# Expert sums in ordered groups, W1's first half in 1 MB loads, and gates behind the one-hot, in a two-block fp32 forward pass

## Chip, cores and metric

The kernel runs on one core of one Trainium2 chip. The metric is the device time of one execution in microseconds.

## What is computed

Two transformer blocks on 512 tokens of width 1024, all in fp32. Only a part of the first block and its hand-over to the second matter here: the hierarchical mixture of experts.

```python
def hier_moe(x, w_group, b_group, w_expert, b_expert, w1, w3, w2):
    ...
    g_logits = (xf @ w_group + b_group).astype(jnp.float32)
    g_sel = jnp.argmax(g_logits, axis=-1)
    ...
    e_top, e_loc = lax.top_k(e_logits, TOP_K_INNER)
    gate = (g_w * jax.nn.softmax(e_top, axis=-1)).reshape(-1)
    ...
        hid = jax.nn.silu(xb @ w1[e]) * (xb @ w3[e])
        return hid @ w2[e]
    ...
    out = jax.ops.segment_sum(ys * row_gate[:, None], row_tok, num_segments=T)
```

There are 4 groups of 8 experts; each token takes 2 experts of one group. An expert has w1 and w3 of 1024 x 512 and w2 of 512 x 1024. The block ends in `h + g2 * hier_moe(...)` and a norm by `final_g`; the second block begins with a layer norm (`ln_in_g_2`, `ln_in_b_2`) and a product with `w_in_2`.

## The kernel before

The program is one long stream per engine. A scheduler sets the order of each engine's instructions from the order in the code, from dependences and from priorities; tiles come from pools that are rings by tag (PG 24 buffers of 512 KB over all partitions, RAW 3 of 1 MB, WH and WL 3 each of 512 KB, SG, SA and PT small ones). A load into a ring waits until the ring's oldest buffer has been read. All loads are issued by SyncE (SP), in order; the gathers of token rows by GpSimd (POOL).

**Mix and norm (L1038 to L1063).** `ev_mix` takes each 128x512 result of the mix product, scales it by g1R and adds it to h on VectorE (DVE), takes the norm's sums, and multiplies h by the row scale sc2R on POOL (L1048). `modulated` then finishes u on DVE and `logits` stores it to u_d (L1063).

**Routing (L1068 to L1213).** Maxima over the logits give the one-hot oh of the two experts of each token. A triangular product gives the rank of each token within its expert; `cnt` and `cnti` hold the largest count. Gates come from sigmoids (ge, gate), and are split into a rounded high part gth and a rest gtl. `slots` (L1153 on) compares ranks with iota to get the one-hot R (L1165); R times pay gives the token of each slot (slots, L1169, then sz, ids, tok), and R times payg its gate (slotg, L1181, then sg, gts in L1183 to L1186). `pair_gather` fetches token rows by tok (L1266). Every engine reads cnti into a register (L1420) and passes a branch (L1424) for the case that an expert has over 64 tokens, which falls back to a loop over single experts (`expert_in`, `expert_out`).

**Experts in pairs (L1367 to L1405, main loop at L1449).** 16 pairs of experts; the first takes columns 0 to 63 of PSUM's partitions, the second 64 to 127. `pair_in` multiplies by W1 and then W3, each in four steps q of two k-slices; the raws of a step are 512 KB per expert, in tags PG, PG, WH, WL. `both` issues the two half-height matmuls (L1371, tile e). After each step it takes one piece of the `beside` stream, the sums of the pair before: `combine` in `outputs` multiplies the yl and yh of that pair by the placing one-hot (L1301, L1302, tile cmb) and adds to h (L1303). `pair_tokens` transposes the next pair's rows (xgt, L1364), `pair_loads` issues the eight w2r loads (L1396, tag PG), `pair_out` transposes the hidden rows (hdt, L1404, copied to hp by ScalarE (ACT), L1406), multiplies by w2r (also L1371), and `outputs` scales the result by gate and g2R (y, L1292) and splits it into yh and yl (L139 on ACT, L140 on DVE).

**End of the loop (j = 16).** The loads of fgR, lng and lnb, and `nav_weights(0).prepare()`, which loads the first raws of the second block's product nav and splits them (L139, L140), stand in the code ahead of the loads and matmuls of w2r of pair 15. Then come the last sums, and the norm chain of the second block: h times fgR (L1939), its statistics, h by lng and lnb (L1223, L1225), transposes xt (L1242) and nav's products.

## Time and profile before

| | |
|---|---|
| median of 3 runs | 3155.69 us (3153.24 to 3157.79) |
| the profiled execution | 3154.16 us, its span 3152.4 us |
| TensorE (PE) | 94% busy, granted clock 0.984 |
| DVE, ACT, POOL | 59%, 36%, 9% busy |
| DMA | 534.17 MB, 527.46 of it on the queue of SP's loads |

The span is cut by the trace into engines' busy times. PE is nearly always busy, but a busy PE isn't one at its peak rate; the loop over the experts runs from about 660 to 1205 us. The table of the profile that shows the span in 40 slices has the transfers at 353 to 377 GB/s in just this stretch, and at 60 to 290 GB/s elsewhere. Times in the rows are in us, unless they are called ns; L is a line of the kernel; `SPq` and `DVEq` are the engines' instruction queues.

### The profile page before, as it was taken

The numbers are of one execution on the slowest core, as the hardware profiler recorded it, in microseconds if no ns is written. First come the engines' busy times: TensorE is split into PE (matmuls) and PEld (weight loads), VectorE is DVE, ScalarE is ACT, GpSimd is POOL, SyncE is SP. The second block draws the span as 40 slices with busy tenths as digits, with TensorE's granted clock in tenths as the row PEclk, the third lists the DMA queues.
The fourth block names the chain that finished last, engine by engine and source line by source line (L and its number), as shares of the span: only waits on it lengthen the run. The fifth ranks groups of instructions, "written<-read, shape, count | busy, mean of one in ns | idle before, by whom it ended". The sixth has DMA issues, their size and how long they took to land.

```text
span 3152.4 us, 36476 instructions
## 1 busy us (share of the span) xinstructions
PE 2970.1 (94%) x13749; PEld 2204.3 (70%) x13749; DVE 1848.6 (59%) x3521; ACT 1131.5 (36%) x1986; POOL 279.6 (9%) x263
## 2 busy tenths in 40 slices
PE   6988999979999998999999999999999999999998
PEld 5766777733333335878867788888888876788887
DVE  6899888633223227555589754434545588764434
ACT  4555244210000003444567332222444576432221
POOL 2133000300000000221000200000221000200000
PEclk9989999989999999999999999999999999999999
DMA  6222756679999995432233623243433234632341
GB/s 222 92 90 65 233 185 195 208 289 353 362 372 377 358 376 193 137 114 94 76 112 111 231 100 107 92 142 100 147 117 101 79 99 116 225 107 93 107 139 62
DMA packets 296257, 534.17 MB, mean 169 GB/s; under 512 B 30279, under 2 KB 172789, under 8 KB 296071
## 3 DMA queue, kind: packets, MB, share of 16 engines
q1 hardware_dynamic: 293480, 527.46, 48.5%
q0 software_dynamic: 2304, 4.20, 0.5%
q8 instruction: 110, 1.80, 0.2%
q14 instruction: 77, 0.62, 0.1%
q10 hardware_dynamic: 286, 0.09, 0.0%
HBM read 486.50 MB, written 44.38 MB: 168 GB/s over the span
## 4 chain that ended last, share of the span: by engine, by line
PE 64%; DVE 7%; issue 3%; DMA 2%; ACT 2%; POOL 1%; SPq 0%; DVEq 0%; POOLq 0%; ACTq 0%
PE e L1371 12%; PE fm L292 9%; PE fm L295 9%; PE fm L293 9%; PE ffo L295 2%; PE ffo L293 2%; PE ffo L292 2%; PE cmb L1301 1%; PE cmb L1302 1%; POOL tl L1634 1%; DVE xT L140 1%; DMA w2r<-in_moe_w_dram 1%; PE mix L292 1%; PE mix L295 1%; PE mix L293 1%
## 5 line engine op out<-in xcount | busy, mean ns | idle before, releaser
L140 DVE TENSOR_TENSOR wl<-raw,wh 128x1024 fp32r<-128x1024 f32 (+3 forms) x403 | 462.3, 1149 | 313.8 <-ACT wh L139 312.2
L139 ACT CAST wh<-raw 128x1024 fp32r<-128x1024 f32 (+3 forms) x403 | 388.6, 966 | 543.0 <-PE fm L295 224.2
L292 PE MATMUL fm<-xT,wh 128*128 128x512 f32 (+1 forms) x1264 | 481.9, 384 | 0.0
L293 PE MATMUL fm<-xT,wl 128*128 128x512 f32 (+1 forms) x1264 | 479.9, 382 | 1.3 <-DVE wl L140 1.3
L295 PE MATMUL fm<-xT,wh 128*128 128x512 f32 (+1 forms) x1264 | 301.9, 381 | 0.0
L1371 PE MATMUL e<-w,xx 128*64 128x512 f32 x1024 | 293.8, 605 | 0.0
L293 PEld LDWEIGHTS fm<-xT,wl 128*128 128x128 f32 x1264 | 238.2, 188 | 46.7 <-DVE wl L140 1.7
L292 PEld LDWEIGHTS fm<-xT,wh 128*128 128x128 f32 x1264 | 238.2, 189 | 45.1
L295 PEld LDWEIGHTS fm<-xT,wh 128*128 128x128 f32 x1264 | 231.6, 188 | 45.5
L1371 PEld LDWEIGHTS e<-w,xx 128*64 128x64 f32 x1024 | 79.2, 137 | 138.6 <-issue 130.0
L293 PE MATMUL fm<-uT,wl 128*128 128x512 f32 (+1 forms) x360 | 145.3, 403 | 3.8 <-DVE wl L140 3.8
L1303 DVE TENSOR_TENSOR h<-h,cmb 128x512 f32<-128x512 f32 x128 | 84.6, 686 | 109.2 <-PE cmb L1302 108.5
L1371 PE MATMUL e<-w2r,hp 128*64 128x512 f32 x512 | 141.9, 607 | 3.6 <-DMA w2r<-in_moe_w_dram 2.1
L292 PE MATMUL fm<-uT,wh 128*128 128x512 f32 (+1 forms) x360 | 145.0, 404 | 0.0
L292 PE MATMUL ffo<-wl,hid 128*128 128x512 f32 x352 | 137.1, 390 | 0.0
L293 PE MATMUL ffo<-wh,hid 128*128 128x512 f32 x352 | 136.9, 389 | 0.0
L1371 PEld LDWEIGHTS e<-w2r,hp 128*64 128x64 f32 x512 | 52.8, 137 | 87.9 <-issue 64.5
L1921 DVE SCALAR_TENSOR_TENSOR ffs<-ffs,fm 128x512 f32<-128x512 f32 x44 | 30.3, 688 | 137.7 <-ACT ffs L1920 137.7
L295 PE MATMUL ffo<-wh,hid 128*128 128x512 f32 x352 | 108.4, 389 | 0.0
L139 ACT CAST yh<-y 128x512 fp32r<-128x512 f32 x32 | 19.8, 618 | 224.2 <-DVE y L1292 224.2
L1923 DVE SCALAR_TENSOR_TENSOR ffs<-ffs,fm 128x512 f32<-128x512 f32 x44 | 30.3, 688 | 114.4 <-PE fm L295 114.4
L1634 POOL TENSOR_TENSOR tl<-ml,tl 128x512 f32<-128x512 f32 x32 | 47.7, 1497 | 554.3 <-DVE tl L1630 540.6
(603 smaller groups left out, 5955.6 us busy)
## 6 DMA issues: line engine op xcount, KB each, us to landing
w<-in_moe_w_dram SPq DMA_DIRECT2D x256, 512.0 KB
raw<-in_w_in_dram SPq DMA_DIRECT2D x71, 1024.0 KB
w2r<-in_moe_w_dram SPq DMA_DIRECT2D x128, 512.0 KB
raw<-in_w_ffn_in_dram SPq DMA_DIRECT2D x44, 1024.0 KB
raw<-in_w_mod_dram SPq DMA_DIRECT2D x42, 512.0 KB
raw<-in_w_ffn_out_dram SPq DMA_DIRECT2D x20, 1024.0 KB
raw<-in_w_out_dram SPq DMA_DIRECT2D x12, 1024.0 KB
t_d<-bg SPq DMA_DIRECT2D x48, 256.0 KB
```

The costliest lines, as they stand in the source:

```text
L139: S.copy(hi, src)
L140: (eng or V).tensor_tensor(lo, src, f(hi), OP.subtract)
L292: PE.matmul(ps, l[0], r[1], start=start and n == 0, stop=False)
L293: PE.matmul(ps, l[1], r[0], start=False, stop=False)
L295: PE.matmul(ps, l[0], r[0], start=False, stop=stop and n == len(pairs) - 1)
L1301: PE.matmul(ps, pl, yl[:, cs], start=True, stop=False)
L1302: PE.matmul(ps, pl, yh[:, cs], start=False, stop=True)
L1303: V.tensor_tensor(h1[i][m], h1[i][m], ps, OP.add)
L1371: PE.matmul(ps[hs], lhs[:, hs], rhs[h], start=start, stop=stop)
L1634: G.tensor_tensor(th, m, th, OP.add)
L1921: V.scalar_tensor_tensor(s, s, 1.0, pgt, OP.add, OP.mult)
L1923: V.scalar_tensor_tensor(s, s, 0.5, pup, OP.mult, OP.mult)
```

## The change

1. In `ev_mix` the row scale by sc2R moves from POOL to DVE.
2. In the routing, `behind(ins, first)` adds an ordering without a wait between two instructions of one engine. With it pay stands behind the one-hot's sum ob, and cnt, ge (and with it the gates) and ex stand behind R. So cnti, the gates and payg come behind R in DVE's order.
3. `combine` becomes a generator that can be sent a matmul behind which its next sum has to stand. `pair_in` asks for 3, 0 | 3, 0, 2, 0 banks of sums after the steps (a bank is two cmb matmuls) in place of one after each step.
4. `pair_in` loads W1 as one 1 MB raw per expert (tag RAW, four k-slices) and two of 512 KB (PG), and W3 as PG, PG, WH, WL. Ahead of the routing's branch SP's order has now 3 loads of 1 MB and 20 of 512 KB for the pairs, before 20 of 512 KB. `expert_in` and `expert_out` in the branch give up RAW for SG and SA buffers.
5. At j = 16 the w2r loads of pair 15 come first; then, pinned in the code's order, fgR, lng, lnb and nav's raws; `prepare` stands behind `pair_out`.

```diff
+    def behind(ins, first):
+
+        tc.add_manual_dep(ins.ins, first.ins.name, mybir.DependencyInfo(mybir.DependencyClass.NoSync, mybir.DependencyReason.DATA),
+                          reason="order")
+        return ins
...
             if hf == 0:
                 hss[i] = pt_("u2", F32, (128, 1024))
-            G.tensor_tensor(hss[i][:, cs], h1[i][hf], sc2R[:, cs], OP.mult)
+            V.tensor_tensor(hss[i][:, cs], h1[i][hf], sc2R[:, cs], OP.mult)
...
-    V.tensor_tensor(ob, oh[:, :, 0], oh[:, :, 1], OP.add)
+    obi = V.tensor_tensor(ob, oh[:, :, 0], oh[:, :, 1], OP.add)
...
-    cnt = const("cnt", [128, 1])
-    V.tensor_reduce(cnt, ps[:, 128:160], AX, OP.max)
-    cnti = const("cnti", [128, 1], I32)
-    V.tensor_copy(cnti, cnt)
+    cntp = ps[:, 128:160]
...
-        V.tensor_tensor(pay[:, :, j], oh[:, :, j], bc(aid[:, :, j], 32), OP.mult)
+        behind(V.tensor_tensor(pay[:, :, j], oh[:, :, j], bc(aid[:, :, j], 32), OP.mult), obi)
...
-            V.tensor_tensor(R[:, :, o:o + n], iota[:, 0:n].unsqueeze(1).to_broadcast([128, 8, n]),
+            Ri = V.tensor_tensor(R[:, :, o:o + n], iota[:, 0:n].unsqueeze(1).to_broadcast([128, 8, n]),
...
-    tok0, ids0, gt0, gates0 = slots(slot_tiles[0], 0, True)
+        return tok, ids, gt, gates, Ri
+
+    tok0, ids0, gt0, gates0, R0i = slots(slot_tiles[0], 0, True)
+    cnt = const("cnt", [128, 1])
+    behind(V.tensor_reduce(cnt, cntp, AX, OP.max), R0i)
+    cnti = const("cnti", [128, 1], I32)
+    V.tensor_copy(cnti, cnt)
     ge = carve("ge", [128, 4, 4])
-    V.tensor_tensor(ge, gl, bc(gm, 4), OP.subtract)
+    behind(V.tensor_tensor(ge, gl, bc(gm, 4), OP.subtract), R0i)
...
-    V.tensor_tensor(ex, m1, m2, OP.subtract)
+    behind(V.tensor_tensor(ex, m1, m2, OP.subtract), R0i)
...
+            after = yield
             for i in range(4):
                 for m in range(2):
                     cs = slice(m * 512, m * 512 + 512)
                     ps = trp("cmb")
                     pl = place[:, i * 128:(i + 1) * 128]
-                    PE.matmul(ps, pl, yl[:, cs], start=True, stop=False)
+                    mm = PE.matmul(ps, pl, yl[:, cs], start=True, stop=False)
+                    if after is not None:
+                        behind(mm, after)
                     PE.matmul(ps, pl, yh[:, cs], start=False, stop=True)
                     V.tensor_tensor(h1[i][m], h1[i][m], ps, OP.add)
-                    yield
-        return combine()
+                    after = yield
+        sums = combine()
+        next(sums)
+        return sums
...
-            PE.matmul(ps[hs], lhs[:, hs], rhs[h], start=start, stop=stop)
+            mm = PE.matmul(ps[hs], lhs[:, hs], rhs[h], start=start, stop=stop)
+        return mm
 
     def pair_in(j, xT, beside):
+
         pss = []
-        for nm in ("moe_w1", "moe_w3"):
+        for n, nm in enumerate(("moe_w1", "moe_w3")):
             W = [I[nm][0, 2 * j + h].rearrange("(p a) n -> p a n", a=8) for h in range(2)]
             ps = mmp("e1")
-            for q in range(4):
+            k = 0
+            for tag, w, banks in ((("RAW", 4, 0), ("PG", 2, 3), ("PG", 2, 0)), (("PG", 2, 3), ("PG", 2, 0), ("WH", 2, 2), ("WL", 2, 0)))[n]:
                 ws = []
                 for h in range(2):
-                    raw = t_([128, 2, 512], F32, ("PG", "PG", "WH", "WL")[q], "w13")
-                    load(raw, W[h][:, 2 * q:2 * q + 2])
+                    raw = t_([128, w, 512], F32, tag, "w13")
+                    load(raw, W[h][:, k:k + w])
                     ws.append(raw)
-                for k in range(2):
-                    both(ps, xT[:, 2 * q + k], [w[:, k] for w in ws], q + k == 0, q + k == 4)
-                next(beside, None)
+                for m in range(w):
+                    mm = both(ps, xT[:, k + m], [r[:, m] for r in ws], k + m == 0, k + m == 7)
+                k += w
+                if beside:
+                    for b in range(banks):
+                        try:
+                            beside.send(None if b else mm)
+                        except StopIteration:
+                            pass
...
-        if j == 16:
-            fgR = row("fgR", I["final_g"])
-            norm, xT = normalizer(I["ln_in_g_2"], I["ln_in_b_2"], rows_of(xres[0]))
-            nav_tm = nav_weights(0).prepare()
         if prev is not None:
-            for _ in beside:
+            for _ in beside or ():
                 pass
-            beside = pair_out(j - 1, prev, pair_loads(j - 1))
+            ws = pair_loads(j - 1)
+            if j == 16:
+                fgR = row("fgR", I["final_g"], True)
+                norm, xT = normalizer(I["ln_in_g_2"], I["ln_in_b_2"], rows_of(xres[0]))
+                nav_tm = nav_weights(0, True)
+            beside = pair_out(j - 1, prev, ws)
+            if j == 16:
+                nav_tm.prepare()
```

How the order moves, first on PE, in one of the first pairs of the loop (w are raws of its W1, e its product, cmb the sums of the pair before). Before, from the pair's first matmul:

```order
L1371 MATMUL e_1441_7154<-w_1442_7155,xx_7086 64x512
L1301 MATMUL cmb_7163<-yl_7147,place_7143 128x512
L1302 MATMUL cmb_7163<-yh_7146,place_7143 128x512
L1301 MATMUL cmb_7175<-yl_7147,place_7143 128x512
L1371 MATMUL e_1441_7154<-w_1443_7157,xx_7086 64x512
L1371 MATMUL e_1441_7154<-w_1442_7155,xx_7086 64x512
L1371 MATMUL e_1441_7154<-w_1443_7157,xx_7086 64x512
L1302 MATMUL cmb_7175<-yh_7146,place_7143 128x512
L1301 MATMUL cmb_7187<-yl_7147,place_7143 128x512
L1302 MATMUL cmb_7187<-yh_7146,place_7143 128x512
```

Now, from the last of the twelve e matmuls in a row here:

```order
L1386 MATMUL e_1483_7334<-w_1487_7349,xx_7266 64x512
L1312 MATMUL cmb_7355<-yl_7327,place_7323 128x512
L1315 MATMUL cmb_7355<-yh_7326,place_7323 128x512
L1312 MATMUL cmb_7359<-yl_7327,place_7323 128x512
L1315 MATMUL cmb_7359<-yh_7326,place_7323 128x512
L1312 MATMUL cmb_7363<-yl_7327,place_7323 128x512
L1315 MATMUL cmb_7363<-yh_7326,place_7323 128x512
L1386 MATMUL e_1483_7334<-w_1491_7367,xx_7266 64x512
L1386 MATMUL e_1483_7334<-w_1492_7369,xx_7266 64x512
```

The groups of three cmb with one or three e rows between them have become groups of six.

On DVE, between the rank and the register load of the branch. Before, with the last payload payg ahead of R:

```order
L1130 TENSOR_REDUCE cnt<-rank_5534 128x1
L1135 TENSOR_TENSOR rt_5554<-carve_4962,rank_5534 128x256
L1132 CAST cnti<-cnt 128x1
L1213 TENSOR_TENSOR payg<-carve_4962,gtl 128x4x32
L1136 TENSOR_REDUCE rank<-rt_5554 128x8
L1165 TENSOR_TENSOR R_5567<-carve_4962,rank 128x8x64 x2
```

Now, with R some twenty rows further up, the part ahead of the register load of cnti:

```order
L150 TENSOR_TENSOR gtl<-carve_4962,gth 128x8
L1223 TENSOR_TENSOR payg<-carve_4962,gth 128x4x32
L1223 TENSOR_TENSOR payg<-carve_4962,gtl 128x4x32
L1223 TENSOR_TENSOR payg<-carve_4962,gth 128x4x32
L1223 TENSOR_TENSOR payg<-carve_4962,gtl 128x4x32
L1189 COPY sg_5614<-slotg_5605 128x64
L1190 TENSOR_TENSOR sg_5614<-sg_5614 128x32
L1192 COPY gts_5559<-sg_5614 64x16 x2
L1444 TENSOR_LOAD cnti
```

The count, the gates (carve is their page), gth, gtl and the four payloads have moved from ahead of R to a place between R and the gate copies gts, ahead of the register load.

On SP, at the loop's end. Before, the last loads of W2 of pair 14 and what follows:

```order
L1396 DMA w2r_9307<-in_moe_w_dram 128x1024
L979 DMA fgR_9345<-in_final_g_dram 128x1024
L979 DMA lng_9347<-in_ln_in_g_dram 128x1024
L979 DMA lnb_9349<-in_ln_in_b_dram 128x1024
L393 DMA raw_9351<-in_w_in_dram 128x4x512
L393 DMA raw_9353<-in_w_in_dram 128x4x512
L1396 DMA w2r_9399<-in_moe_w_dram 128x1024
L1396 DMA w2r_9401<-in_moe_w_dram 128x1024
```

Now, the last loads of W2 of pair 15 and what follows:

```order
L1420 DMA w2r_9519<-in_moe_w_dram 128x1024
L988 DMA fgR_9521<-in_final_g_dram 128x1024
L988 DMA lng_9523<-in_ln_in_g_dram 128x1024
L988 DMA lnb_9525<-in_ln_in_b_dram 128x1024
L400 DMA raw_9527<-in_w_in_dram 128x4x512
L400 DMA raw_9529<-in_w_in_dram 128x4x512
L348 DMA raw_9938<-in_w_in_dram 128x8x256
```

The eight w2r loads of pair 15, which stood behind the rows of the norm and two raws of nav, now stand ahead of them.

## Rows read from the trace of the kernel before

**Rows 1.** DMA view, 900 to 1100 us; the GB/s line has 40 slices of 5 us.

```profile
GB/s 394 419 406 415 342 229 372 407 411 410 410 351 246 387 405 414 408 410 307 262 389 409 415 407 408 308 261 381 397 415 414 409 283 257 387 419 410 410 410 310
DMA packets 20842, 74.53 MB, mean 373 GB/s; under 512 B 2671, under 2 KB 2671, under 8 KB 20833
```

**Rows 2.** Windows of 2 us in one pair: busy us by engine, PEclk, DMA share, GB/s.

```profile
908.00:910.00 2.00, 2.00 (x8) 0.67 (x6) 0.14 (x1) 0.00 (x0) 0.00 (x0) 1.00 1.04 422
...
924.00:926.00 2.00, 2.00 (x8) 0.81 (x6) 0.97 (x2) 0.00 (x0) 0.00 (x0) 1.00 0.71 193
...
928.00:930.00 2.00, 2.00 (x9) 0.77 (x8) 0.27 (x1) 0.90 (x2) 0.34 (x1) 1.00 0.46 84
```

**Rows 3.** Waits of SP's queue, 640 to 1240 us: total us, times, longest.

```profile
SPq L1382 <- PE e L1371: 166.9, 35, 8.7
```

**Rows 4.** The same view, of 922 to 926 and of 926 to 930 us.

```profile
SPq L1382 <- PE e L1371: 7.3, 1, 7.3
...
SPq L1382 <- PE e L1371: 3.6, 1, 3.6
```

**Rows 5.** PE's timeline of one pair: start, us, engine, line, operation, count, [idle before].

```profile
910.12 1.04 PE L1371 MATMUL e<-w,xx 128*64 128x512 f32 x2
912.12 0.50 PE L1301 MATMUL cmb<-yl,place 128*128 128x512 f32 x1 [0.96 <-DVE yl L140]
...
913.33 1.93 PE L1371 MATMUL e<-w,xx 128*64 128x512 f32 x6
915.19 0.50 PE L1302 MATMUL cmb<-yh,place 128*128 128x512 f32 x1
...
916.08 1.07 PE L1371 MATMUL e<-w,xx 128*64 128x512 f32 x2
...
929.55 7.09 PE L1371 MATMUL e<-w,xx 128*64 128x512 f32 x32
936.47 8.57 PE L1371 MATMUL e<-w2r,hp 128*64 128x512 f32 x32
944.47 1.04 PE L1371 MATMUL e<-w,xx 128*64 128x512 f32 x2
```

**Rows 6.** PE's timeline at pair 0's second product.

```profile
698.55 7.09 PE L1371 MATMUL e<-w2r,hp 128*64 128x512 f32 x32 [0.68 <-ACT hp L1406]
```

**Rows 7.** PE's and DVE's timelines at the loop's end; one window of 10 us.

```profile
1194.82 10.86 PE L1371 MATMUL e<-w2r,hp 128*64 128x512 f32 x32 [2.13 <-DMA w2r<-in_moe_w_dram]
...
1194.29 3.50 DVE L140 TENSOR_TENSOR wl<-raw,wh 128x1024 fp32r<-128x1024 f32 x3 [1.21 <-ACT wh L139]
...
1212.94 1.22 DVE L1939 TENSOR_TENSOR h<-h,fgR 128x1024 f32<-128x1024 f32 x1
...
1210.00:1220.00 10.00, 3.24 (x13) 2.13 (x13) 9.54 (x19) 3.28 (x7) 1.41 (x2) 0.84 0.00 2
```

**Rows 8.** DVE's groups of 600 to 660 us: busy us, mean ns, idle before.

```profile
L1213 DVE TENSOR_TENSOR payg<-carve,gth 128x128 fp32r<-128x128 f32 x2 | 0.6, 284 | 0.0
```

**Rows 9.** Timeline of all engines, 651 to 668 us.

```profile
657.50 0.35 DVE L1186 COPY gts<-sg 64x16 f32<-64x16 f32 x2
...
662.65 4.30 DVE L1285 TENSOR_TENSOR place<-carve,rows 128x512 fp32r<-128x512 f32 x7 [4.80 <-DVEq L1424]
662.66 1.94 PE L1364 MATMUL xgt<-ident,xg 128*128 128x128 f32 x8 [5.76 <-DVEq L1424]
662.73 2.85 SPq L1382 DMA_DIRECT2D w<-in_moe_w_dram  x6
```

**Rows 10.** Line L1424, the branch: ns min/median/max, first and last start.

```profile
L1424 PEldq COMPARE_BRANCH  x1: 3352/3352/3352, 654.0 to 654.0; - x1
...
L1424 DVEq COMPARE_BRANCH  x1: 72/72/72, 658.1 to 658.1; - x1
L1424 DVEq EVENT_SEMAPHORE  x1: 21/21/21, 662.5 to 662.5; - x1
```

**Rows 11.** Line L1048; DVE's groups of 600 to 660 us; one window of 10 us.

```profile
L1048 POOL TENSOR_TENSOR u<-h,sc2R x8: 1279/1290/2372, 602.9 to 632.3; 128x512 f32<-128x512 f32 x8
...
L1043 DVE TENSOR_TENSOR mixt<-mix,g1R 128x512 f32<-128x512 f32 x8 | 5.3, 684 | 3.4 <-PE mix L295 3.4
...
620.00:630.00 10.00, 8.08 (x56) 6.25 (x56) 9.56 (x24) 1.37 (x4) 1.82 (x2) 1.00 0.56 179
```

More of the change, by code (lines that the diff above doesn't have):

```diff
@@ L373, in build, with __init__ @@
     class TM:
-        def __init__(self, kt, W, c0, n, name="tm", lead=0, tail=0):
+        def __init__(self, kt, W, c0, n, name="tm", lead=0, tail=0, pinned=False):
+            self.pinned = pinned
             self.kt, self.W, self.c0, self.n, self.name, self.lead, self.tail = kt, W, c0, n, name, lead, tail
@@ L392, in fetch @@
                 self.raw[k0] = t_([128, g, n], F32, "RAW", "raw")
-                load(self.raw[k0], self.W[k0 * 128:(k0 + g) * 128, self.c0:self.c0 + n].rearrange("(k p) n -> p k n", p=128))
+                ins = load(self.raw[k0], self.W[k0 * 128:(k0 + g) * 128, self.c0:self.c0 + n].rearrange("(k p) n -> p k n", p=128))
+                if self.pinned:
+                    tc.keep_in_program_order(ins)
             return self.raw[k0]
@@ L1186, in gates @@
                 V.tensor_copy(d, s)
-        return tok, ids, gt, gates
-    tok0, ids0, gt0, gates0 = slots(slot_tiles[0], 0, True)
+        return tok, ids, gt, gates, Ri
[4 more added lines that the diff above has]
+    V.tensor_copy(cnti, cnt)
     ge = carve("ge", [128, 4, 4])
-    V.tensor_tensor(ge, gl, bc(gm, 4), OP.subtract)
+    behind(V.tensor_tensor(ge, gl, bc(gm, 4), OP.subtract), R0i)
     S.activation(ge, ge, AF.Sigmoid, bias=shiftc)
@@ L1322, in expert_in @@
             for q in range(4):
-                raw = t_([128, 2, 512], F32, "RAW", "w13")
-                load(raw, W[q * 256:(q + 1) * 256, :].rearrange("(k p) n -> p k n", p=128))
                 hi = t_([128, 2, 512], F32R, "WH", "wh")
                 lo = t_([128, 2, 512], F32R, "WL", "wl")
-                split(hi, lo, raw)
+                for k in range(2):
+                    raw = sg("w13")
+                    load(raw, W[(2 * q + k) * 128:(2 * q + k + 1) * 128, :])
+                    split(hi[:, k], lo[:, k], raw)
                 mmk(ps, [((xh[:, 2 * q + k], xl[:, 2 * q + k]), (hi[:, k], lo[:, k])) for k in range(2)],
@@ L1340, in expert_out @@
         for k in range(4):
-            raw = t_([128, 1024], F32, "RAW", "w2r")
-            load(raw, W2[k * 128:(k + 1) * 128, :])
-            hi = t_([128, 1024], F32R, "WH", "wh")
-            lo = t_([128, 1024], F32R, "WL", "wl")
-            split(hi, lo, raw)
+            ks = slice(k * 128, k * 128 + 128)
+            hi = t_([128, 2, 512], F32R, "WH", "wh")
+            lo = t_([128, 2, 512], F32R, "WL", "wl")
             for m in range(2):
-                cs = slice(m * 512, m * 512 + 512)
-                ks = slice(k * 128, k * 128 + 128)
-                mm3(py[m], (hp[:, 0, ks], hp[:, 1, ks]), (hi[:, cs], lo[:, cs]), k == 0, k == 3)
+                raw = sa("w2r")
+                load(raw, W2[ks, m * 512:m * 512 + 512])
+                split(hi[:, m], lo[:, m], raw)
+                mm3(py[m], (hp[:, 0, ks], hp[:, 1, ks]), (hi[:, m], lo[:, m]), k == 0, k == 3)
         return py
@@ L1412, in pair_out, with nav_weights @@
         return outputs(py, gt0[:, j:j + 1], rows0[:, :, j])
-    def nav_weights(l):
-        return TM(8, I["w_in_2"][l], 1024, 512, "nav", lead=3)
+    def nav_weights(l, pinned=False):
+        return TM(8, I["w_in_2"][l], 1024, 512, "nav", lead=3, pinned=pinned)
     g2R = row("g2R", mod_d[3])
@@ L1424, in more @@
         with tc.If(most > base):
-            tok, ids, gt, gates = slots(slot_tiles[1], base, False)
+            tok, ids, gt, gates, _ = slots(slot_tiles[1], base, False)
             gates()
@@ L1445, in build @@
     nav_tm = None
-    beside = iter(())
+    beside = None
     prev = None
```

## The prediction

> **What bounds the kernel now.** The change touches the stretch from about 600 to 1225 us, so I read that stretch and nothing else. First the DMA view of the expert loop [rows 1]: 74.53 MB in 200 us, a mean of 373 GB/s, and rates per 5 us that swing between 229 and 419. A stage that was simply bound by its transfers would not swing. Then the windows of 2 us inside one pair of experts [rows 2]: 422 GB/s at the pair's start, and two holes of 193 and 84 GB/s. Then what the queue that issues the loads waits for [rows 3, 4]: over the loop it stands 166.9 us behind matmuls of L1371, in 35 waits, and in this one pair 7.3 and 3.6 us, at the two holes. Two of the four steps of W1 and of W3 load into rings of three buffers (tags WH and WL), and each pair needs four of each; so the fourth waits until TensorE has read the first, and the 20 or so loads behind it wait too. Last, TensorE's own timeline of the pair [rows 5]: it repeats every 34.35 us (a pair's first e matmuls start at 910.12, the next pair's at 944.47), and it hardly idles, but it loses time in three ways. It waits 0.96 us for yl before the first sum. The 32 matmuls on w2r take 8.00 us from 936.47, where the 32 before them took 6.92 (929.55 to 936.47): 1.08 lost on late rows. And each switch between expert matmuls and other work costs: six e matmuls from 913.33 to 915.19 take 1.86 us, where six at 6.92/32 = 0.216 are 1.30, and the three cmb behind them take 0.89 where three at 0.216 are 0.65. That is 0.56 + 0.24 = 0.80 us for each such change and back, eight times in a pair.
>
> So both sides of the loop are loose: the transfers because of holes that the rings make, TensorE because of stalls that these holes and the switches make. Two floors follow.
>
> **The loop, part by part.** *Floor of the transfers.* A pair moves 74.53 MB x 34.35/200 = 12.80 MB, gathers included [rows 1, 5]; the change moves the same bytes. At 410 GB/s, a value between the full rates of [rows 1, 2], that is 31.2 us; at 422 it is 30.3. *Floor of TensorE.* The sums now come in groups of 6, 6 and 4 matmuls instead of 3, 1, 3 and so on, so the eight interruptions become five: 34.35 − 3 x 0.80 = 31.95. Grouped behind twelve e matmuls, yl is ready: −0.96. If rows are on time: −1.08. One thing is added: hdt now stands right before the w2r matmuls, so hp has to be waited for, as it is for pair 0 today, 0.68 us [rows 6]. Together 31.95 − 0.96 − 1.08 + 0.68 = 30.6 us.
>
> *What lets the loop come to its floors.* W1's first half now goes as two 1 MB loads into the RAW ring of three, and only two halves instead of four go into WH and WL. Four fewer buffers per pair are asked of rings that are too short, and the loads before the routing's branch grow from 20 of 512 KB (10.5 MB) to 20 of these and 3 of 1 MB (13.6 MB), counted in the instruction order of SP: more than one pair ahead. A lead of that size isn't used up by a difference of 0.6 us per pair in fourteen pairs, so TensorE's floor is as likely as that of the transfers. I take 31.0, between 30.6 and 31.4. Fourteen periods (w2r of pair 0 to w2r of pair 14) x (34.35 − 31.0) = **46.9 us gained**.
>
> *Last pair.* Today the loads of w2r for pair 15 stand behind those of the final norm and of nav, and the matmuls wait 2.13 us and then take 10.86 [rows 7]; issued first, they take 6.92 after 0.68. 12.99 − 7.60 = **5.4 gained**. The loads that now come later (raw of nav, 1 MB each) are wanted by the splits only; they are covered by those 7 us and the sums behind.
>
> **What it costs.** *Routing.* The gates, payloads and counts leave VectorE's queue ahead of the one-hot R and stand behind it. R starts a little earlier (two payloads of 0.28 us and small work [rows 8], partly in gaps while it waits for others: 0.6). But then the work has to be done between R and the gates' copies gts, ending at 657.85 today [rows 9], and VectorE's passage through the branch stands behind gts. There it is what all wait for: VectorE's branch stands at 658.1 and its next event at 662.5, 4.4 us, and only then do the transposes (5.76 us idle), place and SP's next loads go on [rows 9, 10]. The work of SLOTG can't start before payg: I count some seven small ops of 0.15 to 0.2 us, two sigmoids on ScalarE with their hand-overs, and four payloads, of which about 2 us hide under the slots matmuls; 3.3 us net on the join. The bounds: −0.6, where all hides, and +5, where the sigmoids' hand-overs lie fully open. By the Trainium skill ("Runtime: NRT & Kernel Launch", Instruction fetch mechanics) a taken branch whose target lies outside the two pages at hand makes the engine fetch the page first. The trace agrees in so far as 4.4 us pass behind VectorE's branch and TensorE's own takes 3.35 [rows 10]; by that rule a branch that is reached later on the last engine moves the join by the full amount. From the rows alone: **+3.3**, once.
>
> *Row scale.* Eight ops of 128x512 go from POOL (1.29 us median) to VectorE, where a multiply of that shape takes 0.68 [rows 11]. The first four lie under the mix matmuls; the rest fall into 620 to 630 us, where VectorE is busy 9.56 of 10 us. There they cost up to 4 x 0.68 = +2.7; where the POOL op was in the chain they give back up to 4 x 0.6 = −2.4. I take **+0.5**.
>
> *Hand-over to block 2.* The three wl splits of nav, 3.50 us, run today in VectorE's wait for the last w2r matmuls [rows 7]. In the new order they stand behind the seventh and eighth sum of the last pair, right ahead of the multiply by fgR (at 1212.94), on an engine that is busy 9.54 of 10 us from 1210 to 1220. Less the little that was idle: **+3.4**. At the least 0, if their rows and casts come at a gap; at the most +6, if the casts on ScalarE (queued behind squares) are waited for as well.
>
> **Sum.** 46.9 + 5.4 − 3.3 − 0.5 − 3.4 = 45.1 gained, on the profiled execution's 3154.16: **3109 us**. The median of the runs is 1.5 us above the profiled one, less than the range.
>
> **The rivals.**
> *Half the gain.* The short rings remain (WH, WL and RAW have three buffers for two loads per pair), and small dips remain between loads. If one hole of some 1.5 us stays, the period is 32.5: 14 x 1.85 = 25.9, minus 1.8 for the rest, 24 gained, 3130. For it: the smaller hole today (3.6 us of waiting [rows 4]) is at the end of W3, where the rings still turn.
> *More.* The routing hides its gates (−0.6, no cost of the row scale) and the period is 30.4: 14 x 3.95 + 0.6 + 5.4 − 3.4 = 57.9, 3096.
> *The mean rate is a ceiling.* If 373 GB/s is what memory gives, the holes only move; the period stays 34.35 and the rest gives −1.8: 3156, no change. Against it: the 422 GB/s of [rows 2] and 5-us rates over 405 in most of [rows 1]. The Trainium skill ("DMA: Bandwidth & Descriptors", Where 436 GB/s comes from) says that loads from memory are bound near 358 GB/s per core; by it 12.80 MB need 35.8 us and nothing could be gained here. The rows hold far more than 358 for ten microseconds on end, so I give it little.
> *Slower: a new wait at the head of SP's queue.* Pair j+1's second 1 MB load takes the buffer of pair j's first W1 half, and some 20 loads stand behind it. It decides by how long that wait lasts. Today 10.9 us of waiting per pair cost 31.2 → 34.35, some 3 us of transfers, since loads in flight cover about 8. A single wait of over 11 us loses more than today; at 12 us the period is 31.2 + 4 = 35.2, and 14 x 0.85 + 1.8 = 13.7 are lost: 3168. Against it: the buffer is free as soon as the first eight W1 steps of a pair are over, 4 us into it, while the ring lets the load before it go a pair earlier.
>
> **How the numbers follow.** A difference of 0.2%, 6.3 us, is what a measurement can tell. Forecast (period 30.6 to 31.5, costs within their bounds, 3098 to 3120): 0.66. Half the gain (3120 to 3140): 0.18. More (below 3098): 0.07. Ceiling: 0.06. New wait: 0.03. Faster 0.91, same 0.06, slower 0.03. The range takes the forecast's, half of "more" and most of the half gain: 3092 to 3134.
>
> **What would show it.** Right: w2r matmuls of successive pairs about 31 us apart; 32 of them in about 7 us with no DMA releaser; cmb in groups of six; SP's waits behind matmuls still long in sum but without holes under 300 GB/s inside a pair, or with holes that TensorE doesn't feel; place and the first transposes at about 666 instead of 662.66; wl x3 between the last sums and fgR. Wrong: a period over 33; DMA rates that never pass 380; e matmuls waiting for w; a join no later than today's; or an extra wait of TensorE between hdt and w2r of over 1 us, since it would count fourteen times.

## The result, and the profile after

| | median | range | ratio to before |
|---|---|---|---|
| before, beside it | 3154.61 us | 3153.24 to 3157.79 (4 runs) | |
| changed | 3101.83 us | 3100.89 to 3107.15 (4 runs) | 0.9835, 95% interval 0.9818 to 0.9852 |

The kernel is 52.8 us faster. The forecast was 45 us, 3109 in a range of 3092 to 3134. The profiled execution took 3102.56 us, its span is 3100.8.

The DMA view of the changed kernel, 900 to 1100 us, answers to [rows 1]:

```profile
GB/s 410 421 406 411 406 409 406 417 415 406 410 401 409 407 416 409 410 407 402 406 420 410 403 411 405 410 407 415 409 409 406 411 412 417 410 411 405 410 413 416
DMA packets 20955, 81.99 MB, mean 410 GB/s; under 512 B 2684, under 2 KB 2684, under 8 KB 19224
```

The swings between 229 and 419 GB/s are gone. No slice is under 401, and the mean went from 373 to 410: the loop now runs at the rate of its transfers. The waits of SP's queue, 640 to 1240 us (us in total, times, longest), answer to [rows 3]:

```profile
SPq L1400 <- PE e L1386: 22.6, 33, 6.5
```

It was 166.9 us. PE's timeline of one pair answers to [rows 5]:

```profile
915.34 1.02 PE L1386 MATMUL e<-w,xx 128*64 128x512 f32 x2
917.50 5.36 PE L1386 MATMUL e<-w,xx 128*64 128x512 f32 x22 [1.14 <-DMA w<-in_moe_w_dram]
922.80 0.50 PE L1312 MATMUL cmb<-yl,place 128*128 128x512 f32 x1
...
924.38 3.65 PE L1386 MATMUL e<-w,xx 128*64 128x512 f32 x16
927.96 0.50 PE L1312 MATMUL cmb<-yl,place 128*128 128x512 f32 x1
...
934.26 1.07 PE L1386 MATMUL e<-w,xx 128*64 128x512 f32 x2
...
936.01 1.93 PE L1386 MATMUL e<-w,xx 128*64 128x512 f32 x6
...
939.64 7.14 PE L1386 MATMUL e<-w2r,hp 128*64 128x512 f32 x32 [0.68 <-ACT hp L1430]
946.55 1.02 PE L1386 MATMUL e<-w,xx 128*64 128x512 f32 x2
```

The pair takes 946.55 − 915.34 = 31.21 us, where it took 34.35. TensorE waits 1.14 us for w, which it did not do before, and 0.68 for hp; the wait for yl is gone and the w2r matmuls take 6.9 us (939.64 to 946.55). So transfers set the pace from here on. From 640 to 1240 us TensorE's waits for w (total us, times, longest) come to:

```profile
PE e L1386 <- DMA w<-in_moe_w_dram: 10.3, 11, 1.4
```

But the first pairs, with the loads' lead still there, are shorter: from hdt to hdt the periods (one per pair) are 27.82, 29.05, 29.06, 30.49 us, and then 31.2 to 31.5 for the next five. The five after these go from 27.5 to 33.8; in the one of 33.8 TensorE first waits 0.46 and 1.35 us for w, and its clock is then granted at a mean of 0.83 from 980 to 990 us, so in part at the lower of its two levels, 1.2 GHz. The first three are TensorE's own time, and it is below the forecast's 30.6.

A balance by marks that both timelines have (before, after, in us):

| mark | before | after | stretch up to it, change |
|---|---|---|---|
| ScalarE copies the logits (lgs) | 642.77 | 642.41 | −0.4 |
| first xgt (the join behind the branch) | 662.66 | 663.87 | +1.6 |
| first w2r matmul of pair 0 | 698.55 | 697.88 | −1.9 |
| first w2r matmul of pair 14 | 1175.84 | 1124.31 | −50.9 |
| end of the w2r matmuls of pair 15 | 1205.68 | 1147.08 | −7.1 |
| first xt | 1218.77 | 1164.59 | +4.4 |
| end of the span | 3152.4 | 3100.8 | +2.6 |

The last line is no effect of the change: over all profiles of this study that stretch is between 1931.9 and 1938.7 us long, with the same instructions in it. The start too moves by some us from run to run.

At the join, the timeline of the changed kernel and the branch's line answer to [rows 9, 10]:

```profile
657.68 0.28 DVE L1223 TENSOR_TENSOR payg<-carve,gtl 128x128 fp32r<-128x128 f32 x1
657.71 2.02 PE L1187 MATMUL slotg<-payg,R 128*128 128x64 f32 x8 [3.48 <-DVE payg L1223]
...
660.25 0.35 DVE L1192 COPY gts<-sg 64x16 f32<-64x16 f32 x2
...
663.87 1.94 PE L1379 MATMUL xgt<-ident,xg 128*128 128x128 f32 x8 [4.14 <-DVEq L1448]
```

```profile
L1448 DVEq COMPARE_BRANCH  x1: 72/72/72, 660.9 to 660.9; - x1
...
L1448 DVEq EVENT_SEMAPHORE  x1: 21/21/21, 663.8 to 663.8; - x1
```

slotg waits 3.48 us for payg, and gts is written 2.75 us later than before. But VectorE's passage takes 2.9 us, not 4.4, so the join comes only 1.2 us later (1.6 counted from lgs, as in the table). The end of the loop, DVE's and PE's timelines, answers to [rows 7]:

```profile
1153.74 2.35 DVE L146 TENSOR_TENSOR wl<-raw,wh 128x1024 fp32r<-128x1024 f32 x2
1156.01 0.68 DVE L1316 TENSOR_TENSOR h<-h,cmb 128x512 f32<-128x512 f32 x1
1156.61 1.22 DVE L146 TENSOR_TENSOR wl<-raw,wh 128x1024 fp32r<-128x1024 f32 x1
1157.74 1.21 DVE L1966 TENSOR_TENSOR h<-h,fgR 128x1024 f32<-128x1024 f32 x1
...
1139.99 7.09 PE L1386 MATMUL e<-w2r,hp 128*64 128x512 f32 x32 [0.68 <-ACT hp L1430]
...
1164.59 1.97 PE L1252 MATMUL xt<-ident,h 128*128 128x128 f32 x8 [11.18 <-DVE h L1235]
```

The w2r matmuls of the last pair are on time. The three wl splits now stand among the last sums, in the chain that xt waits for, 11.18 us instead of 6.76.

### The profile page after: what moved, and what is told of

Read it like the earlier page. It is cut to its first block, busy times and chain, and to the rows that moved or that the text cites. A ratio compares the mean times of both kernels' runs of the same rounds, so it can differ in the third digit from the quotient of the medians.

```text
span 3100.8 us, 36570 instructions
## 1 busy us (share of the span) xinstructions
PE 2910.5 (94%) x13749; PEld 2192.2 (71%) x13749; DVE 1843.1 (59%) x3529; ACT 1131.1 (36%) x1986; POOL 266.9 (9%) x255
## 4 chain that ended last, share of the span: by engine, by line
PE 53%; DMA 12%; DVE 7%; issue 3%; ACT 2%; POOL 1%; SPq 0%; DVEq 0%; POOLq 0%; ACTq 0%
PE fm L298 9%; PE fm L299 9%; PE fm L301 9%; DMA w<-in_moe_w_dram 8%; DMA w2r<-in_moe_w_dram 4%; PE e L1386 3%; PE ffo L301 2%; PE ffo L298 2%; PE ffo L299 2%; POOL tl L1661 1%; DVE wl L146 1%; PE mix L298 1%; PE mix L301 1%; PE mix L299 1%; DVE xT L146 1%
## 5 line engine op out<-in xcount | busy, mean ns | idle before, releaser
L1386 PE MATMUL e<-w,xx 128*64 128x512 f32 x1024 | 260.1, 604 | 10.3 <-DMA w<-in_moe_w_dram 10.3
L1386 PE MATMUL e<-w2r,hp 128*64 128x512 f32 x512 | 115.1, 596 | 10.1 <-ACT hp L1430 10.1
L1947 ACT ACTIVATE ffs<-fm 128x512 f32<-128x512 f32 x44 | 26.3, 598 | 188.6 <-PE fm L301 188.6
L1386 PEld LDWEIGHTS e<-w2r,hp 128*64 128x64 f32 x512 | 41.3, 136 | 72.9 <-issue 58.7
```

The lines of the kernel that those rows point to most:

```text
L1386: mm = PE.matmul(ps[hs], lhs[:, hs], rhs[h], start=start, stop=stop)
L1947: S.activation(s, pgt, AF.Tanh, scale=0.5)
```

## The experiments

**The two halves of the loop's edit, one at a time.** `ungroup` keeps the new buffers and gives the sums out as before; `oldbuf` keeps the groups and loads in the old sizes and tags.

```diff
 ungroup
...
                 for m in range(w):
-                    mm = both(ps, xT[:, k + m], [r[:, m] for r in ws], k + m == 0, k + m == 7)
+                    both(ps, xT[:, k + m], [r[:, m] for r in ws], k + m == 0, k + m == 7)
+                    if beside and m % 2:
+                        next(beside, None)
...
 oldbuf
...
-(("RAW", 4, 0), ("PG", 2, 3), ("PG", 2, 0)), (("PG", 2, 3), ("PG", 2, 0), ("WH", 2, 2), ("WL", 2, 0))
+(("PG", 2, 0), ("PG", 2, 0), ("WH", 2, 3), ("WL", 2, 0)), (("PG", 2, 3), ("PG", 2, 0), ("WH", 2, 2), ("WL", 2, 0))
```

> The changed kernel with its new buffers and loads, but one bank of sums after each two k-slices, as before, with no ordering. Theory A (grouping lowered TensorE's time per pair from about 32.3 to 29.0 us, and the loop now runs at the transfers' 31.2): TensorE is the bound again, a period of 32.3 to 33.3 us, the median about 3134 us (3127 to 3142), SP's waits behind e matmuls and holes in the transfer rate come back. Rival B (the new buffers did it all): unchanged, 3102, rate flat at 410 GB/s. Rival C (grouping did it all): the loop's gain is lost, about 3150.

> The changed kernel with grouped sums, but each pair's W1 and W3 in raws of 512 KB with the tags PG, PG, WH, WL as before. Theory A (the rings make holes in the transfers that a faster TensorE only narrows): period about 33, about 3137 us, holes under 300 GB/s inside a pair. Rival C (the holes were slack that a slow TensorE left; with grouped sums the buffers come free early enough): period 31.2 to 31.5, about 3110 us, of which 7 to 8 us are the 3.1 MB that are no longer loaded ahead of the branch.

Measured: `ungroup` 3132.11 us (3129.48 to 3134.46), ratio 0.9918 (0.9901 to 0.9934); `oldbuf` 3113.09 us (3111.29 to 3119.97), ratio 0.9868 (0.9851 to 0.9884). From w2r of pair 0 to w2r of pair 14 before took 477.3 us, `ungroup` 452.3, `oldbuf` 436.1, the changed kernel 426.4. `ungroup` is as theory A had it: 32.46 us per pair in most pairs, TensorE waiting for yl (over 640 to 1240 us) and never for w:

```profile
PE cmb L1312 <- DVE yl L146: 22.6, 14, 2.2
```

Its order on TensorE is not that of before, though: without an ordering the scheduler made e groups of 1, 11, 1, 3, 1 and 15 matmul rows, where before had 1 and 3 in turn. So the 25.0 us between before and `ungroup` can't all be put down to the buffers. Its DMA view, 950 to 1150 us, has holes again:

```profile
GB/s 412 400 410 410 419 333 357 415 411 410 406 388 406 407 406 409 410 419 315 399 413 408 410 410 335 359 401 414 403 414 417 303 360 419 411 409 407 407 411 406
```

`oldbuf` went against theory A and with rival C. Same rings, same tags as before the change, and yet the DMA view, 950 to 1100 us, is flat:

```profile
GB/s 409 406 409 411 404 405 413 409 407 408 407 411 404 375 405 415 411 407 405 409 412 403 378 401 416 411 404 412 406 410 407 410 410 411 406 412 410 411 402 411
DMA packets 17058, 61.02 MB, mean 407 GB/s; under 512 B 2180, under 2 KB 2180, under 8 KB 17051
```

From the second to the twelfth its periods are 31.3 to 32.0 us, with one of 32.8. So short rings alone did not make the holes of [rows 2]. They were the idle time of transfers that were ahead of a slow TensorE: once that frees the buffers sooner, the same rings keep the queue full. The new buffers are worth 3113.09 − 3101.83 = 11.3 us by the medians and 9.7 on this stretch, of which 7.5 lie in its first four periods. An estimate for the lead of 3.1 MB at 410 GB/s is 7.7, which agrees, but the lead and the size and tags of the loads were not tried one at a time.

**TensorE's own time, and what a switch costs.** `less` takes W3's last four slices from W1's raws, so that transfers can't be the bound; `less_odd` also moves the first and third group of sums between the two halves of a slice.

```diff
 less
...
+                if tag == "RAW":
+                    first = []
+                ws = [t[:, k - 4:k - 2] for t in first] if n and k >= 4 else []
+                for h in range(2 - len(ws)):
...
 less_odd, at a group's place
+                    mm = PE.matmul(ps[0:CAP], lhs[:, 0:CAP], ws[0][:, m], start=start, stop=stop)
+                    for b in range(banks):
+                        mm = beside.send(None if b else mm)
+                    behind(PE.matmul(ps[CAP:128], lhs[:, CAP:128], ws[1][:, m], start=start, stop=stop), mm)
```

> The changed kernel, but the last four k-slices of W3 are multiplied from W1's two 1 MB raws instead of W3's own: 2.1 of 12.6 MB per pair are not moved, so the product is another one; TensorE's work is the same. It shows TensorE's own time per pair. Theory A: with the transfers' floor at 26 us every period is TensorE's, 28.2 to 29.0 us (the first pairs of the changed kernel take 29.05, and here the transposes stand after an even number of halves), w2r of pair 0 to w2r of pair 14 in 395 to 406 us instead of 426.4, about 3075 to 3082 us. Rival (TensorE's floor is the 30.6 of the forecast): 428 us, unchanged at 3102.

> As less (the last four k-slices of W3 from W1's raws), but the first and third group of sums stand between the two halves of a k-slice, so that the e groups have 11, 9, 7 and 5 matmul rows instead of 12, 8, 8 and 4; the number of switches is the same. Theory P (the two halves of 64 columns run at the same time, and what a switch costs is above all a half that is left without its partner, about 0.43 us): four odd groups, 4 x 0.43 = 1.7 us more per pair than less, some 24 us over 14 pairs. Rival Q (each switch between the two kinds of matmul costs 0.8 us, whatever stands around it): the same time as less within 3 us.

Measured: `less` 3068.0 us (2 runs), `less_odd` 3088.31 us (2 runs). The periods are 27.82 to 27.86 us in thirteen pairs of `less`, and 29.53 or 29.54 in `less_odd`: 1.69 more, where theory P said 1.7 and rival Q nothing. `less` came out below even theory A's range: 388.9 us from w2r of pair 0 to w2r of pair 14, where 395 to 406 were expected. As it loads 2.1 MB less per pair and its periods drop to these, the steady 31.2 us of the changed kernel are the transfers', not TensorE's. PE's timeline of `less` shows a group of 12 rows (24 records) and one of 8:

```profile
905.77 5.32 PE L1386 MATMUL e<-w,xx 128*64 128x512 f32 x24
911.01 0.51 PE L1312 MATMUL cmb<-yl,place 128*128 128x512 f32 x1
...
912.62 3.65 PE L1386 MATMUL e<-w,xx 128*64 128x512 f32 x16
916.20 0.50 PE L1312 MATMUL cmb<-yl,place 128*128 128x512 f32 x1
```

And that of `less_odd` one of 11 rows (20 and 2 records; L1412 is the half that was moved ahead of the sums, L1415 its partner behind them):

```profile
914.75 4.46 PE L1386 MATMUL e<-w,xx 128*64 128x512 f32 x20
919.04 1.02 PE L1412 MATMUL e<-w,xx 128*64 128x512 f32 x2
919.99 0.50 PE L1312 MATMUL cmb<-yl,place 128*128 128x512 f32 x1
...
921.58 0.64 PE L1415 MATMUL e<-w,xx 128*64 128x512 f32 x1
921.59 0.64 PE L1386 MATMUL e<-w,xx 128*64 128x512 f32 x1
```

Eleven rows take 919.99 − 914.75 = 5.24 us, as long as twelve (911.01 − 905.77 = 5.24). The two halves run at the same time on their 64 columns (the partner that was left behind and a half of the next slice start at 921.58 and 921.59); a half whose partner stands on the other side of a group takes the time of both. A whole group costs little: 16 matmuls take 3.58 us, 0.12 over 16 x 0.216. Before the change, the e groups ahead of the last one had 1 and 3 rows, all odd, eight times a pair; now only the two around xgt are. In `less` these too are even, and its period is 1.2 us below the 29.05 of the changed kernel's own first pairs. The changed kernel shows the same by itself. In its pair 1 the scheduler left xgt whole, behind a group of 4 rows, and only from pair 2 on it stands between groups of 1 and 3 rows; the first period is 27.82 us, the next 29.05:

```profile
721.52 1.94 PE L1386 MATMUL e<-w,xx 128*64 128x512 f32 x8
723.39 1.16 PE L1379 MATMUL xgt<-ident,xg 128*128 128x128 f32 x8
```

Two halves without a partner (0.86 us) and one more switch (0.36) are 1.22.

`less_odd` also shows again whose holes they are. TensorE waits for a load once in its whole loop, for 1.6 us, and its DMA view, 900 to 1000 us (slices of 2.5), has deeper holes than before (136 at the lowest in the same slices); it also has 2.1 MB less to move per pair:

```profile
GB/s 423 111 187 400 416 403 410 410 400 411 415 410 411 26 252 395 413 398 400 415 406 411 411 421 351 59 298 406 411 403 408 419 406 406 410 424 282 56 375 401
```

**The routing.** `oldroute` has all `behind` of the routing taken out and the old order of the lines.

```diff
...
-    behind(V.tensor_tensor(ge, gl, bc(gm, 4), OP.subtract), R0i)
+    V.tensor_tensor(ge, gl, bc(gm, 4), OP.subtract)
...
```

> The changed kernel, with the routing in the order of before (gates, payloads and count ahead of the one-hot R, no ordering). One look at the path from ScalarE's copy of the logits (lgs) to the first transposes xgt: 21.5 us in the changed kernel, 19.9 before. Theory (the gates behind R delay slotg and with it VectorE's branch): back to 19.9 or, as the branch took 2.9 us and not 4.4, down to 18.4; the time 1.5 to 3 us less, about 3100, which one look can't tell from 3102. Rival (the join hangs on something else, such as the gathers): 21.5.

One run: 3103.8 us. From lgs to xgt 645.88 to 665.74 = 19.86 us, as before, where nine kernels with the new order took 21.5 to 21.8 us (two others with the old order: 20.2 and 20.3). The theory holds, with the longer passage of 4.4 us. So gates behind the one-hot cost some 1.6 us on this path (1.2 to 1.9 over these kernels). From the join to w2r of pair 14 it was 2.6 us shorter than the changed kernel too. In its second pair xgt stands whole (a period of 27.86 us in place of 29.04), and the loads behind the join come in another order; what each of these gives was not tried.

**The row scale.** `pool` has that one line of `ev_mix` back on POOL.

```diff
-            V.tensor_tensor(hss[i][:, cs], h1[i][hf], sc2R[:, cs], OP.mult)
+            G.tensor_tensor(hss[i][:, cs], h1[i][hf], sc2R[:, cs], OP.mult)
```

> The changed kernel with the row scale of the mix back on POOL. From the first mixt to ScalarE's copy of the logits lgs it took 41.84 us before and 41.82 in the changed kernel: 41.8 again, if the row scale is off the path on either engine. Rival (VectorE's extra 5.5 us cost something that other changes gave back): 41.3 or less.

One run: 3100.37 us, 599.09 to 640.93 = 41.84 us. It makes no difference that this path shows; in other kernels with the changed row scale it took 41.8 or 42.5 us.

**The end of the loop.** `oldend` restores it; `tail` keeps the new order of loads and holds pair 15's y on VectorE until nav's three splits are done.

```diff
 oldend
...
+        if j == 16:
+            fgR = row("fgR", I["final_g"])
+            norm, xT = normalizer(I["ln_in_g_2"], I["ln_in_b_2"], rows_of(xres[0]))
+            nav_tm = nav_weights(0).prepare()
...
 tail
...
+            yi = V.scalar_tensor_tensor(y[:, cs], py[m], gtc, g2R[:, cs], OP.mult, OP.mult)
+            if nav_tm:
+                behind(yi, nav_tm.last)
...
```

> The changed kernel, with the end of the loop as before: norm rows and nav's raws loaded and split ahead of pair 15's w2r. By the marks of the two kernels (start of w2r of pair 14 to the first xt: 42.9 us before, 40.3 after) it should cost 2 to 3 us: 12 to 13 us for pair 15's w2r including its wait in place of 7.1, and 13.1 in place of 17.5 us from there to xt. Rival (in a loop whose transfers are late anyway the w2r loads come later still): 45 us and more.

> The changed kernel, with the three splits of nav's first raws put ahead of pair 15's scaled rows y on VectorE, so back into its wait for the last w2r matmuls. Theory (in the changed kernel they stand among the last sums and cost the norm chain what they take): from the end of the last w2r matmul to the first xt transposes 13.1 us as before the change in place of 17.5, the median 4 us below the changed kernel, about 3098. Rival (the chain waits for nav's raws or for ScalarE's squares anyway): 17 us, 3102.

`oldend`, one run: 3099.61 us; from w2r of pair 14 to xt 1123.47 to 1164.18 = 40.7 us against 40.3. So the new end is worth 0.4 us in this one run, not 2 to 3. The w2r matmuls show why the two sides nearly cancel (the wait of 1.85 us and 10.79 us here, 0.68 and 7.09 there, and then 13.1 and 17.5 to xt):

```profile
1140.32 10.79 PE L1386 MATMUL e<-w2r,hp 128*64 128x512 f32 x32 [1.85 <-DMA w2r<-in_moe_w_dram]
```

`tail` went against both its theory and its rival: 3105.23 us (3104.05 to 3106.37), ratio 0.9838 (0.9822 to 0.9855), 20.4 us from the last w2r to xt. Its timelines of SP, ACT and DVE:

```profile
1136.98 1.65 SPq L400 DMA_DIRECT2D raw<-in_w_in_dram  x2
...
1148.63 1.99 ACT L145 CAST wh<-raw 128x1024 fp32r<-128x1024 f32 x2 [7.33 <-DMA raw<-in_w_in_dram]
...
1149.71 2.36 DVE L146 TENSOR_TENSOR wl<-raw,wh 128x1024 fp32r<-128x1024 f32 x2 [8.64 <-ACT wh L145]
```

The raws are issued at 1136.98 and can be cast only at 1148.63, behind w2r loads that are still being moved. VectorE waits 8.64 us for them. With transfers as the bound, loads issued later come later; w2r on time and the splits in VectorE's old gap did not go together here.

**More lead.** `freeif` takes the rings WH and WL out of the branch's fallback, so that their first loads no longer wait for the join.

```diff
...
-                hi = t_([128, 2, 512], F32R, "WH", "wh")
-                lo = t_([128, 2, 512], F32R, "WL", "wl")
+                    hi, lo = sa("wh", 512, F32R), sa("wl", 512, F32R)
...
```

> The changed kernel, with the fallback in the branch using small buffers in place of the rings WH and WL, so that the first loads of these rings can be issued ahead of the branch: 26 loads of 512 KB and 3 of 1 MB in place of 20 and 3, 3.1 MB more. Theory (once the lead is used up, the loop is bound by transfers at 410 GB/s, and these stand idle during the routing): 3.1 MB / 410 = 7.7 us less from the join to the last load, TensorE's waits for w vanish for about two more pairs, the median about 3094 to 3096. Rival (the lead isn't worth its bytes, since the rings refill it within the first pairs): within 2 us of 3102.

Measured: 3099.43 us (3096.89 to 3101.59), ratio 0.9821 (0.9805 to 0.9838); these runs can't tell it from the changed kernel. From the join to w2r of pair 14 it gained 2.5 us, not 7.7, and here too xgt stands whole in the second pair (27.81 us in place of 29.04), which may be a part of it. SP's timeline, and its queue's waits from 640 to 690 us, show where the rest went:

```profile
637.67 4.40 SPq L1417 DMA_DIRECT2D w2r<-in_moe_w_dram  x4
670.27 0.34 SPq L1397 DMA_DIRECT2D w<-in_moe_w_dram  x1
671.98 2.59 SPq L1417 DMA_DIRECT2D w2r<-in_moe_w_dram  x4
...
SPq L1397 <- PE e L1383: 24.8, 5, 14.8
```

More is loaded ahead, and then SP issues nothing until 670.27, since the next buffers are full and come free when pair 0 is under way. The changed kernel begins at 663.93; from 664 to 680 us it moves 5.28 MB and `freeif` 3.45, so 1.8 of the 3.1 MB are made up by then. My expectation left out that a lead is bounded by buffers, not by time.

**All that helped, together.** `best` is `oldroute`, `freeif` and `tail`; `best2` is `oldroute`, `freeif` and, in place of `tail`, nav's first splits on POOL.

```diff
-                nav_tm.prepare()
+                nav_tm.prepare(G)
```

> The changed kernel with all three: old order of the routing, rings WH and WL free of the branch, nav's splits ahead of y. If the three gains add: 4.4 + 7.7 + 1.6 = 13.7 us below the changed kernel, about 3088. If a bound is met in between (TensorE's own 29 us per pair): still 3088 to 3091, since transfers need 31.2.

> The changed kernel with the old order of the routing, the rings WH and WL free of the branch (as in freeif), and nav's three first splits on POOL instead of VectorE. From the marks of the runs before: 3.0 us in the loop (freeif), 1.6 on the way to the join (oldroute), and 3.5 of the 4.4 us in the norm chain, since three splits of 2.5 us on POOL begin at about 1150 and end at about 1158, ahead of the first xt at 1160: some 8 us below the changed kernel, 3094 (3092 to 3097). Rival: nav's first products wait for POOL's splits, or VectorE runs slower beside POOL, and the chain's 17.5 us from the last w2r matmul to xt stay: 3097 to 3098.

`best`: 3100.22 us (3095.84 to 3100.82), ratio 0.9818 (0.9802 to 0.9834); the gains didn't add, as `tail`'s part is a loss, and those of `freeif` and `oldroute` overlap (457.9 us from the join to w2r of pair 14 in either, and 458.0 in both together). `best2`: 3095.55 us (3094.76 to 3097.68, 5 runs), ratio 0.9809 (0.9796 to 0.9822), the fastest kernel here that loads all weights, 6.3 us below the changed one by medians, though the two intervals still touch. It is in the expected range in part by luck: from lgs to xt, where all its edits lie, it takes 518.7 us, the changed kernel 522.2, `oldroute` 518.0, so 3.5 us of the difference are there and the rest lies ahead of lgs and behind xt. Its own edit gave little: from the last w2r to xt 16.9 us, where 14 were hoped for. Its POOL and DVE timelines:

```profile
1148.13 8.93 POOL L146 TENSOR_TENSOR wl<-raw,wh 128x1024 fp32r<-128x1024 f32 x3 [118.14 <-ACT wh L145]
...
1149.37 2.21 DVE L1962 TENSOR_TENSOR h<-h,fgR 128x1024 f32<-128x1024 f32 x1
...
1154.79 2.29 DVE L1966 TENSOR_TENSOR msq<-msq,bmv 128x1 f32<-128x1 f32 x1
```

While POOL splits, VectorE's multiply by fgR takes 2.21 us in place of 1.21, and a one-column op 2.29 in place of 0.15: the rival of that expectation.

## Why the prediction was right, and where not

1. **What bounds the kernel.** Half wrong. The forecast read the two holes in [rows 2] and SP's waits in [rows 3, 4] as the cause ("holes that the rings make"). `oldbuf` has the old rings and no slice under 375 GB/s, `less_odd` has the new ones and deep holes: they are what is left when TensorE is the slower side. What the short rings cost beside the old order of sums stays open, since `ungroup` has other e groups than before. [rows 5] had said so: TensorE idled 0.96 us for yl and lost 1.08 on late rows, and the other 32.3 of the 34.35 us were its own work.
2. **The transfers' floor.** Right: 31.2 us at 410 GB/s, and 31.21 measured in the pair above at a mean of 410.
3. **TensorE's floor.** The step that failed is "each switch costs 0.80 us, eight become five, 30.6 us". It was 29.05, and 27.84 with even groups. The 0.56 us that I saw on six e matmuls in [rows 5] was no price of a switch but a half without its partner, 0.43 us of it, and the groups of one and three rows all had one. Six of eight such groups went, which is 2.6 us, and three switches at some 0.36 (0.12 on the e side, 0.24 on the cmb side) are 1.1: together 3.7 in place of 2.4. With that, 32.31 − 3.7 + 0.68 = 29.3 us, 0.2 above the measured period.
4. **The loop.** Forecast 46.9, measured 50.9, and the agreement is in part luck. The forecast counted from 34.35 us, one pair; the fourteen periods before have a mean of 34.09. So the old stretch was put 3.6 us too long (480.9 against 477.3) and the new one 7.6 too long (434.0 against 426.4). Its mean period is 30.46, which is that of the rival "More" and not the 31.0. The steady periods are a little above 31.0; the first four, 27.8 to 30.5, are below it, since there TensorE's floor counts.
5. **The first pairs.** A term that was not in the sum: from the join to w2r of pair 0 it is 1.9 us shorter. In `oldbuf`, without the larger lead, it is 35.7 us, near the 35.9 of before. That points to the lead, but the clock has a part: behind the idle time of the routing it is granted at 0.50 (the lower level, 1.2 GHz), and it rises between 665 and 670 us, where its mean is 0.77 before, 0.74 after and 0.60 in `oldbuf`. W3's rows of pair 0, behind the rise, take 14.64, 13.88 and 14.04 us.
6. **The last pair and the hand-over.** Forecast 5.4 gained and 3.4 lost; measured 7.1 and 4.4. About 2.2 of the 7.1 are w2r of pair 14, on time in `oldend` as well, so they belong to the loop, and 4.9 are left. The rest nets 0.4 us in one run, not 2.0. Of the 4.4, the splits make the 3.4 of the forecast (from the last w2r matmul to the multiply by fgR 10.66 us in place of 7.26). The other 1.0 was in no term: two one-column operations of the chain on VectorE took 0.70 and 0.64 us, beside work of POOL, where they took 0.16 each before:

```profile
1162.34 1.39 POOL L1589 TENSOR_TENSOR nasm<-nab,colmask 128x256 f32<-128x256 f32 x2 [127.35 <-DVE rst L196]
...
1162.37 0.70 DVE L197 SCALAR_TENSOR_TENSOR rst<-rst,msq 128x1 f32<-128x1 f32 x1
1163.10 0.64 DVE L198 SCALAR_TENSOR_TENSOR rst<-rst,rsy 128x1 f32<-128x1 f32 x1
```
7. **Routing.** Forecast +3.3, measured +1.6. The delay of gts was 2.75 us plus a start that was 0.4 earlier, close to the forecast; VectorE's passage through the branch gave 1.5 back, which I had taken as fixed at 4.4. So a branch that was reached later did not move the join by the full amount.
8. **Row scale.** Forecast +0.5 (from −2.4 to +2.7), measured 0.0.
9. **The rivals.** The period of 32.5 of "half the gain" did come about, but in `ungroup` and from TensorE, not from a hole that stayed. The mean rate was no ceiling: 410 GB/s against 373. By the Trainium skill ("DMA: Bandwidth & Descriptors", Where 436 GB/s comes from) it would have been near 358; the run differs, and the measurement decides. The new wait at the head of SP's queue did not show: 22.6 us of waits behind e matmuls in all.
10. **The signs.** Two of them came out the other way. TensorE does wait for w, 10.3 us in 11 waits, which was to be a sign of being wrong; and SP's waits behind matmuls, which were to stay long in sum, fell from 166.9 to 22.6 us. Both say that the transfers became the slower side in most pairs, where the forecast had held the two floors equally likely. The join came at 663.87, not at 666.

## What to carry to other kernels

A hole in the transfers with a wait of the load queue at it doesn't tell which side is slow: ask first whether the compute engine waits for those loads, and if it hardly does, shorten its work before its rings are made deeper. Where two half-height matmuls run side by side, count rows between interruptions: an even number keeps the halves together, and each odd group cost 0.42 us here. A scheduler may split such a group for a few transposes without being asked (xgt from pair 2 on, 1.2 us a pair), so read the order that it made. A lead of loads is worth what the buffers hold, and work that is ordered behind it comes late by the queue in front of it.

## What was not expected of the hardware

- Two matmuls with 64 columns each, in the two halves of the columns, run at the same time: the two rows of a slice take 0.86 us (four records at 0.216). A row that is left alone takes as long as the two, so eleven rows took the 5.24 us of twelve. The Trainium skill ("TensorEngine Tiling (Array Packing)", Tiling Modes) says that tiles work independently and that a change of the mode drains the engine; the runs show the first with this price, and some 0.36 us there and back for the switch as a whole; what of it is the drain was not tried.
- VectorE's passage through the same branch, with the same instruction after it, took 4.4 to 4.8 us in the four kernels with the old order of the routing and 2.9 to 3.2 in the nine with the new. By the Trainium skill ("Runtime: NRT & Kernel Launch", Instruction fetch mechanics) a taken branch whose target lies outside the two pages at hand has to fetch the target's page first. Whether the place of the branch in a page makes the difference wasn't tried.
- Beside 128x1024 splits on POOL (8.93 us for three, 2.98 each), a 128x1024 multiply on VectorE went from 1.21 to 2.21 us in `best2`.
